# A two-layer hybrid decoder step on one core: two plain tile pairs open each feed-forward block, the first block's norm sums move into its third tile, and the embedding transposes move behind the gate's first tile

## The chip, the cores and the metric

The kernel runs on one core of one Trainium2 chip. Five engines run side by side, each with its own list of instructions in a fixed order: TensorE (PE in the profile, its weight loads PEld), VectorE (DVE), ScalarE (ACT), GpSimd (POOL) and SyncE (SP, which issues most DMAs here). [...] An engine that waits for one instruction's input holds back everything behind it in its own list. The metric is the device time of one execution in microseconds. The median of three runs is 2243.88 us (2239.72 to 2243.95).

## The reference

Two layers. Each layer is a feed-forward block with half weight, a mixing block (a state-space scan beside window attention), a second feed-forward block with half weight, and a gated per-layer embedding. 512 prompt tokens and 32 sample tokens go through together, 544 in all; the model is 1024 wide, the feed-forward blocks 2752.

```python
def _rmsnorm(x, w):
    y = xf * lax.rsqrt(jnp.mean(xf * xf, axis=-1, keepdims=True) + RMS_EPS)
    return (y * w).astype(x.dtype)

def _swiglu(x, w1, w3, w2):
    return (jax.nn.silu(x @ w1) * (x @ w3)) @ w2

h = h + 0.5 * _swiglu(_rmsnorm(h, g_ffn1), w1_a, w3_a, w2_a)
...
h = h + mix
h = h + 0.5 * _swiglu(_rmsnorm(h, g_ffn2), w1_b, w3_b, w2_b)
gate = sigmoid(_rmsnorm(h, g_ple) @ w_ple_gate)
h = h + gate * (pe @ w_ple_proj)
```

## The kernel before

The residual stream `h` stays in SBUF, 128 partitions by 8 chunks of 544 tokens. Every matrix product is made of three products of halves: an operand is split into a high part (a cast by ScalarE: `wh`, `qh`, `XH`) and the rest (a subtraction by VectorE: `wl`, `ql`, `XL`), and TensorE adds up high times high, high times low and low times high. A matmul has 272 columns, half of the tokens. So `xgemm`, one tile of 128 output columns over all 1024 inputs, is 8 x 3 x 2 = 48 matmuls, and the weights of each tile have to be loaded (`raw`), cast by ScalarE and subtracted by VectorE (`split`, L98 to L102) before they can be used.

**The norm.** `Norm` splits `h` times the gain into `XH` and `XL`. The factor of each token is applied later, to the products. GpSimd and ScalarE add up the squares into `acc`. `sums` (L166) lets TensorE add them over the partitions, VectorE makes `v` of them (L173, L174), and GpSimd raises it to the power -1/2 (`rt`, L175). `spread` (L177) lets TensorE copy the factors to all partitions, and ScalarE copies them to `Rb` (L184, L185). No product can be multiplied by its factor before `Rb` is there.

**A feed-forward block** (`ffn`) has 21 tile pairs and a remainder of 64 columns; a pair is 128 columns of w1 and the same 128 of w3. One pair and the remainder are computed plainly (`plain`): three `xgemm` tiles, `p1`, `p3` and the remainder `ps`. The other 20 pairs go through `pair`, which takes the four quarters of w1, w3 and of the input (two halves of the inputs by two halves of the tokens), and needs 7 products of quarters in place of 8. It pays with sums of weight quarters on VectorE and GpSimd (`q1` L338, L339, L340, L345), seven weight splits, and sums and differences of the results in VectorE (`v` L364 and L366, `c2`, `t`). A block pair is 84 matmuls; a plain pair is 96. The products read sums of input quarters that `block_sums` makes once for each block: ScalarE writes `Y`, VectorE makes four sums (L269 to L272), ScalarE casts them and VectorE subtracts (L276, L277), into `T` and into the part of `XH` and `XL` that the plain tiles have read. `Y` shares its buffers with `U`.

**Down.** The gated products go to sets `U` of four pairs. While the next set is computed, the down projection of the last one is added to `h`, two of eight output tiles for each pair: `plain_down` for the set of the plain pair and the remainder (10 matmuls and a weight unit of 2 x 128 columns for each tile), `down` for a set of four (24 matmuls and a weight unit of 4 x 128). So there are five sets of block pairs, and the first runs beside the small `plain_down`.

**Names for what follows.** I call the L366 instruction of a pair its second `v`. It frees the bank in which TensorE goes on (`T,wh` rows), so the distance from one second `v` to the next is the time of a pair. The stretch from the first tile of a block to its first second `v` is the opening. The blocks are counted FFN 1 to 4.

**The first block.** In layer 0 the tiles are begun while the input still comes in (`begun`); there the program calls `sums` after the second tile and `spread` after the third, while the other three blocks call them after the first and the second.

**The gate** (`ple`). `ple_prep` loads this layer's embedding `pt`, turns it with ten transposes on TensorE and splits it into `EH` and `EL`. It is called ahead of `ple`, so its transposes stand in TensorE's list ahead of the gate's first tile. The buffer of `pt` lies where the feed-forward block's buffers were, so its load waits for the end of that block. After the gate's first tile come `norm.sums`, the first projection of the embedding, and `norm.spread`.

**The order.** The code above is recorded, and a scheduling layer then sets the order of each engine's list; a list can therefore stand in another order than the code. Six `raw` buffers are shared by all weight units that are not `ra` (four more).

Of the kernel before, what the change touches and what calls it, by code (L numbers as in the profile page):

```python
# [9 lines left out]
F32 = mybir.dt.float32  # L10
F32R = mybir.dt.float32r
AF = mybir.ActivationFunctionType
ALU = mybir.AluOpType
# [3 lines left out]
DEPTH = 2  # L17
# [5 lines left out]
N = NP + NS  # L23
HN = N // 2
KU = 4
KD = DM // 128
# [13 lines left out]
def hymba_step(ctx: ExitStack, tc: tile.TileContext, I, O):  # L40
# [74 lines left out]
    def terms3(p, k, xh, xl):  # L115
        wh, wl = p[k // KU]
        k %= KU
        return [(wh[:, k, :], xh), (wh[:, k, :], xl), (wl[:, k, :], xh)]

    def gemm(groups):  # L120
        ps = (bank(), bank())
        n = len(groups)
        for gi, terms in enumerate(groups):
            for a in range(2):
                for i, (lhsT, rhs) in enumerate(terms):
                    PE.matmul(ps[a][:, 0:HN], lhsT, rhs[:, a * HN:(a + 1) * HN], start=gi == 0 and i == 0,  # L126
                              stop=gi == n - 1 and i == len(terms) - 1)
        return ps

    def xgemm(p):  # L130
        return gemm([[t for k in range(KD) for t in terms3(p, k, XH[:, k, :], XL[:, k, :])]])

    def xtile(w, c0):
        return xgemm(piece(w, 0, c0, KD))
# [99 lines left out]
    def ffn(g, w1, w3, w2, begun=None):  # L234
# [5 lines left out]
        with tc.tile_pool(name="ffn", bufs=2, reuse_waits="tile") as fp:  # L240
            T = fp.tile([128, 6, KU, HN], F32R, tag="T", name="T", bufs=1)

            def uset():
                return fp.tile([128, 2, PH, N], F32R, tag="U", name="U")

# [35 lines left out]

            def plain():
                U = uset()
                p1 = xgemm(first[0])
                if not begun:
                    norm.sums()
                p3 = xgemm(first[1])
                if begun:
                    norm.sums()
                else:  # L290
                    norm.spread()
                c0 = NJ * 128
                ps = xgemm(load_piece(
                    [(lambda t: t[:, :, 0:FREM], w1[:, c0:DFF].rearrange("(k p) m -> p k m", p=128)),
                     (lambda t: t[:, :, FREM:128], w3[:, c0:DFF].rearrange("(k p) m -> p k m", p=128))], KD))
                if begun:
                    norm.spread()
                sums = block_sums()
                s = act(p1)
                u = fp.tile([128, N], F32, tag="c2", name="u")  # L300
                for a in range(2):
                    V.tensor_tensor(u[:, HALF[a]], p3[a][:, 0:HN], s[:, HALF[a]], op=ALU.mult)
                keep(U, 0, u)
                b = fp.tile([64, N], F32, tag="c2", name="b64")
                for a in range(2):
                    A.copy(b[:, HALF[a]], ps[a][64:128, 0:HN])
                s = act(ps, 64)
                u = fp.tile([64, N], F32, tag="c2", name="ur")
                V.tensor_tensor(u, b, s[0:64, :], op=ALU.mult)
                A.copy(U[0:64, 0, 1, :], u)  # L310
                V.tensor_sub(U[64:128, 0, 1, :], u, U[0:64, 0, 1, :].bitcast(F32))
                return U, sums

            def plain_down(U, m):
                cs = slice(m * 128, (m + 1) * 128)
                parts = [(lambda t: t[:, 0, :], w2[0:128, cs])]
                parts += [(lambda t, a=a: t[a * 64:(a + 1) * 64, 1, :], w2[NJ * 128:DFF, cs]) for a in range(2)]
                p = split(raw_unit(parts), 2)
                terms = terms3([p], 0, U[:, 0, 0, :], U[:, 1, 0, :])
                terms += [(p[i][:, 1, :], U[:, 0, 1, :]) for i in range(2)]  # L320
                add_down(m, gemm([terms]), 0.25)

            def add_down(m, ps, f):
# [53 lines left out]
                V.tensor_tensor(c2, c2, th, op=ALU.mult)  # L377
                keep(U, i, c2)

            def down(j0, U, m):  # L380
                src = w2[j0 * 128:(j0 + PH) * 128, m * 128:(m + 1) * 128].rearrange("(k p) m -> p k m", p=128)
                p = load_piece([(lambda t: t, src)], PH)
                add_down(m, gemm([[t for k in range(PH) for t in terms3(p, k, U[:, 0, k, :], U[:, 1, k, :])]]), -0.25)

            U, sums = plain()
            last = lambda m, U=U: plain_down(U, m)
            for j0 in range(1, NJ, PH):
                U = uset()
                for i in range(PH):
                    pair(j0 + i, sums, U, i)  # L390
                    for m in range(2 * i, 2 * i + 2):
                        last(m)
                last = lambda m, U=U, j0=j0: down(j0, U, m)
            for m in range(KD):
                last(m)

# [734 lines left out]
    def ple(l, P, lp, E, last):  # L1131
        EH, EL = E
# [17 lines left out]
        for m in range(KD):  # L1150
            pg = xgemm(first if m == 0 else piece(wg, 0, m * 128, KD))
            if m == 0:
                norm.sums()
            p = piece(wpj, 0, m * 128, 2)
            pe = gemm([[t for k in range(2) for t in terms3(p, k, EH[:, k, :], EL[:, k, :])]])
            if m == 0:
# [43 lines left out]
    for l in range(DEPTH):  # L1200
# [7 lines left out]
        mix(l, P)  # L1208
        ffn(P["g2"], I["w1_b"][l], I["w3_b"][l], I["w2_b"][l])
        with tc.tile_pool(name="ple", bufs=2, reuse_waits="tile") as lp:  # L1210
            E = ple_prep(l, lp)
            Pn = params(l + 1) if l + 1 < DEPTH else None
            ple(l, P, lp, E, l == DEPTH - 1)
        P = Pn


# [62 lines left out]
```

## Time and profile before

| | |
|---|---|
| median of 3 runs | 2243.88 us |
| the profiled execution, its own time | 2237.84 us |
| its span | 2236.0 us |
| granted TensorE clock in that execution | 0.98 |
| DVE busy | 1808.7 us, 81% |
| ACT busy | 963.0 us, 43% |
| POOL busy | 701.2 us, 31% |

In the rows of the profile an engine's busy time is the union of its instructions. "x" is a count. A row of the stretches has for each engine the busy time and the number of instructions, then the granted TensorE clock, the busy share of the DMA engines, and GB/s. A row of a group has the line of the kernel, the engine, the operation, what it writes and reads, the shape, the count, the busy time, the mean ns of one, and the idle time before it with what ended it.

### The profile page before, as it was taken

The numbers are of one execution on the slowest core, as the hardware profiler recorded it, in microseconds if no ns is written. First come the engines' busy times: TensorE is split into PE (matmuls) and PEld (weight loads), VectorE is DVE, ScalarE is ACT, GpSimd is POOL, SyncE is SP. The second block draws the span as 40 slices with busy tenths as digits, with TensorE's granted clock in tenths as the row PEclk, the third lists the DMA queues.
The fourth block names the chain that finished last, engine by engine and source line by source line (L and its number), as shares of the span: only waits on it lengthen the run. The fifth ranks groups of instructions, "written<-read, shape, count | busy, mean of one in ns | idle before, by whom it ended". The sixth has DMA issues, their size and how long they took to land.

```text
span 2236.0 us, 43393 instructions
## 1 busy us (share of the span) xinstructions
PE 2132.3 (95%) x16706; PEld 2085.0 (93%) x16706; DVE 1808.7 (81%) x3282; ACT 963.0 (43%) x1784; POOL 701.2 (31%) x601
## 2 busy tenths in 40 slices
PE   7889999999999899999988999999999998999999
PEld 7889999998899899999988999999888888999998
DVE  7998987589878898986587889875987888988854
ACT  6344443444454444444363344443443543444343
POOL 5233331233533333322133333322334433323220
PEclk9999999999999999999999999999998999999999
DMA  5343332313252333332323333332223323333222
GB/s 143 101 118 95 91 104 72 80 50 86 58 139 63 99 95 100 91 90 73 87 64 100 101 95 92 93 81 70 59 76 90 94 74 104 91 103 96 77 70 76
DMA packets 401211, 197.89 MB, mean 88 GB/s; under 512 B 40270, under 2 KB 400358, under 8 KB 401004
## 3 DMA queue, kind: packets, MB, share of 16 engines
q1 hardware_dynamic: 399420, 194.93, 31.9%
q8 instruction: 132, 2.16, 0.4%
q14 instruction: 75, 0.61, 0.1%
q10 hardware_dynamic: 1584, 0.18, 0.0%
HBM read 187.56 MB, written 9.53 MB: 88 GB/s over the span
## 4 chain that ended last, share of the span: by engine, by line
PE 69%; DVE 18%; issue 4%; POOL 4%; DMA 3%; ACT 2%; POOLq 0%; SPq 0%; DVEq 0%; ACTq 0%
PE ps L126 35%; PE ps L354 28%; DVE wl L101 3%; DVE ql L101 2%; DVE CV L654 1%; POOL th L250 1%; DMA raw<-in_w_a 1%; POOL q L338 1%; DVE ra L345 1%; DMA raw<-in_w_b 1%; DVE wk L517 1%; PE ps L900 1%; DVE c L377 1%; DVE th L249 1%; POOL raw L339 1%
## 5 line engine op out<-in xcount | busy, mean ns | idle before, releaser
L126 PE MATMUL ps<-U,wh 128*128 128x272 f32 x2752 | 525.5, 288 | 0.0
L100 ACT CAST wh<-raw 128x512 fp32r<-128x512 f32 (+1 forms) x448 | 264.8, 596 | 445.6 <-PE ps L126 246.1
L126 PEld LDWEIGHTS ps<-U,wh 128*128 128x128 f32 x2752 | 434.4, 189 | 0.0
L126 PE MATMUL ps<-U,wl 128*128 128x272 f32 x1408 | 401.5, 288 | 0.0
L101 DVE TENSOR_TENSOR wl<-raw,wh 128x512 fp32r<-128x512 f32 (+1 forms) x448 | 312.9, 701 | 73.5 <-ACT wh L100 65.9
L126 PE MATMUL ps<-XH,wh 128*128 128x272 f32 x1184 | 352.3, 300 | 8.9 <-DVE wk L517 4.3
L126 PE MATMUL ps<-XL,wh 128*128 128x272 f32 x1184 | 345.8, 294 | 3.0 <-DVE XL L155 2.9
L126 PE MATMUL ps<-XH,wl 128*128 128x272 f32 x1152 | 336.9, 293 | 0.0
L126 PEld LDWEIGHTS ps<-U,wl 128*128 128x128 f32 x1408 | 265.4, 189 | 0.0
L354 PE MATMUL ps<-T,qh 128*128 128x272 f32 x1280 | 246.4, 289 | 0.5 <-ACT qh L100 0.4
L126 PEld LDWEIGHTS ps<-XH,wh 128*128 128x128 f32 x1184 | 227.8, 193 | 14.7 <-DVE wk L517 4.7
L338 POOL TENSOR_TENSOR q<-raw 128x512 f32<-128x512 f32 x80 | 124.9, 1561 | 355.0 <-DMA raw<-in_w_b 177.5
L126 PEld LDWEIGHTS ps<-XL,wh 128*128 128x128 f32 x1184 | 228.8, 193 | 4.8 <-DVE XL L155 4.3
L126 PEld LDWEIGHTS ps<-XH,wl 128*128 128x128 f32 x1152 | 222.6, 193 | 0.0
L375 POOL TENSOR_TENSOR t<-t,Rb 128x272 f32<-128x272 f32 x80 | 68.6, 857 | 463.2 <-DVE t L374 402.5
L354 PEld LDWEIGHTS ps<-T,qh 128*128 128x128 f32 x1280 | 202.0, 189 | 0.9 <-ACT qh L100 0.9
L354 PE MATMUL ps<-XH,wh 128*128 128x272 f32 x640 | 186.0, 291 | 11.3 <-ACT v L362 8.6
L354 PE MATMUL ps<-T,ql 128*128 128x272 f32 x640 | 186.1, 292 | 7.5 <-DVE ql L101 7.5
L354 PE MATMUL ps<-XH,ql 128*128 128x272 f32 x640 | 188.5, 294 | 4.1 <-DVE ql L101 4.1
L354 PE MATMUL ps<-XH,qh 128*128 128x272 f32 x640 | 187.8, 293 | 4.4 <-DVE c L368 4.4
L354 PE MATMUL ps<-XL,qh 128*128 128x272 f32 x640 | 188.4, 294 | 0.0
L101 DVE TENSOR_TENSOR ql<-ra,qh 128x512 fp32r<-128x512 f32 x160 | 181.9, 1137 | 7.7 <-ACT qh L100 0.7
(389 smaller groups left out, 5071.1 us busy)
## 6 DMA issues: line engine op xcount, KB each, us to landing
raw<-in_w_a SPq DMA_DIRECT2D x168, 256.0 KB
raw<-in_w_b SPq DMA_DIRECT2D x168, 256.0 KB
ra<-in_w_a SPq DMA_DIRECT2D x80, 256.0 KB
ra<-in_w_b SPq DMA_DIRECT2D x80, 256.0 KB
raw<-in_w_in SPq DMA_DIRECT2D x60, 256.0 KB
raw<-in_w_ple_gate SPq DMA_DIRECT2D x32, 256.0 KB
raw<-in_w_in SPq DMA_DIRECT2D x32, 128.0 KB
raw<-in_w_out SPq DMA_DIRECT2D x32, 128.0 KB
```

The costliest lines, as they stand in the source:

```text
L100: A.copy(wh[:, 0:n, :], raw[:, 0:n, :])
L101: V.tensor_sub(wl[:, 0:n, :], raw[:, 0:n, :], wh[:, 0:n, :].bitcast(F32))
L126: PE.matmul(ps[a][:, 0:HN], lhsT, rhs[:, a * HN:(a + 1) * HN], start=gi == 0 and i == 0, stop=gi == n - 1 and i == len(terms) - 1)
L249: V.scalar_tensor_tensor(th[0:np_, :], th[0:np_, :], 1.0, t1[0:np_, :], op0=ALU.add, op1=ALU.mult)
L250: G.tensor_tensor(th[0:np_, :], th[0:np_, :], Rb[0:np_, :], op=ALU.mult)
L338: G.tensor_tensor(q1, a21, a22, op=ALU.add)
L339: G.tensor_tensor(a21, a21, a11, op=ALU.add)
L345: V.tensor_tensor(a12, a12, a11, op=ALU.add)
L354: PE.matmul(ps[:, 0:HN], lhsT, rhs, start=start and k == 0 and n == 0, stop=k == KU - 1 and n == 2, skip_group_check=not start)
L375: G.tensor_tensor(t[:, HALF[1]], t[:, HALF[1]], Rb[:, HALF[1]], op=ALU.mult)
L377: V.tensor_tensor(c2, c2, th, op=ALU.mult)
L517: V.scalar_tensor_tensor(P3[:, kv, q, k0:256], sc[kv][:, q * 256:q * 256 + nk], rq[j][:, i, kv:kv + 1], bias_p[:, k0:256], op0=ALU.mult, o ...
```

## The change

It does three things.

1. `plain` computes two tile pairs plainly, pair 0 and pair 1. Its tiles are now `p1`, `p3`, `pn`, `pm` and the remainder. Nineteen pairs are left for `pair`, in sets of 3, 4, 4, 4 and 4. `plain_down` has three units of 128 rows of w2 (16 matmuls for each tile, before 10), the first `down` has three (18 matmuls, before 24), and the first set's three pairs share the eight `plain_down` tiles as 2, 3 and 3.
2. In the first block `sums` is called in the middle of the third tile, and `spread` behind it.
3. `ple_prep` is called behind the gate's first tile and its `sums`.

```diff
-    def gemm(groups):
+    def gemm(groups, mid=None):
         ps = (bank(), bank())
         n = len(groups)
         for gi, terms in enumerate(groups):
+            if gi and mid:
+                mid()
...
-    def xgemm(p):
-        return gemm([[t for k in range(KD) for t in terms3(p, k, XH[:, k, :], XL[:, k, :])]])
+    def xgemm(p, mid=None):
+        return gemm([[t for k in range(k0, k0 + KU) for t in terms3(p, k, XH[:, k, :], XL[:, k, :])]
+                     for k0 in range(0, KD, KU)], mid)
...
+                def product(i, p1, p3):
+                    s = act(p1)
+                    u = fp.tile([128, N], F32, tag="c2", name="u")
+                    for a in range(2):
+                        V.tensor_tensor(u[:, HALF[a]], p3[a][:, 0:HN], s[:, HALF[a]], op=ALU.mult)
+                    keep(U, i, u)
+
                 p1 = xgemm(first[0])
                 if not begun:
                     norm.sums()
                 p3 = xgemm(first[1])
                 if begun:
-                    norm.sums()
+                    pn = xgemm(piece(w1, 0, 128, KD), norm.sums)
+                    norm.spread()
                 else:
                     norm.spread()
+                    pn = xgemm(piece(w1, 0, 128, KD))
+                product(0, p1, p3)
+                pm = xgemm(piece(w3, 0, 128, KD))
                 c0 = NJ * 128
                 ps = xgemm(load_piece(
...
-                if begun:
-                    norm.spread()
+                product(1, pn, pm)
                 sums = block_sums()
-                s = act(p1)
-                u = fp.tile([128, N], F32, tag="c2", name="u")
-                for a in range(2):
-                    V.tensor_tensor(u[:, HALF[a]], p3[a][:, 0:HN], s[:, HALF[a]], op=ALU.mult)
-                keep(U, 0, u)
...
-            for j0 in range(1, NJ, PH):
+            for j0, n in ((2, PH - 1), (5, PH), (9, PH), (13, PH), (17, PH)):
                 U = uset()
-                for i in range(PH):
+                for i in range(n):
+                    ms = range(KD * i // n, KD * (i + 1) // n)
                     pair(j0 + i, sums, U, i)
-                    for m in range(2 * i, 2 * i + 2):
+                    for m in ms:
                         last(m)
...
             pg = xgemm(first if m == 0 else piece(wg, 0, m * 128, KD))
             if m == 0:
                 norm.sums()
+                EH, EL = ple_prep(l, lp)
...
-            E = ple_prep(l, lp)
```

The change moves the lists as follows at three places. Line numbers shift by up to ten (L101 stays; L173, L269, L366 become L176, L272, L375).

**VectorE at the opening of FFN 2.** Before, from the last weight split of the opening tiles on; `Y` and `T` are the sums of `block_sums`, `t_8495` is the first product times `Rb`:

```order
L101 TENSOR_TENSOR wl<-ra,wh 128x512
L271 TENSOR_TENSOR Y<-Y 128x4x272
L173 TENSOR_SCALAR v<-ps 128x4
L174 TENSOR_SCALAR v<-ps 32x1
L272 TENSOR_TENSOR Y<-Y 128x4x272
L277 TENSOR_TENSOR T<-Y,T 128x1088 x3
L340 TENSOR_TENSOR ra<-ra,q_8534 128x512
```

Now, from the same `v` on; `t_8461` and `t_8599` are the first products of the two plain pairs, times `Rb`:

```order
L177 TENSOR_SCALAR v<-ps 32x1
L101 TENSOR_TENSOR wl<-raw,wh 128x512 x3
L143 TENSOR_TENSOR t_8461<-ps,Rb 128x272 x2
L252 SCALAR_TENSOR_TENSOR th<-th,t_8461 128x544
L101 TENSOR_TENSOR wl<-ra,wh 128x512
L292 TENSOR_TENSOR u<-ps,th 128x272 x2
L143 TENSOR_TENSOR t_8599<-ps,Rb 128x272
L349 TENSOR_TENSOR ra<-ra,q_8659 128x512
L263 TENSOR_TENSOR U<-u,U 128x544
L143 TENSOR_TENSOR t_8599<-ps,Rb 128x272
L252 SCALAR_TENSOR_TENSOR th<-th,t_8599 128x544
L272 TENSOR_TENSOR Y<-Y 128x4x272
```

The sums of the input quarters stood ahead of the first product that needs `Rb`; now all of them stand behind the first plain pair and most of the second. FFN 3 and 4 have the same order.

**GpSimd at the opening of FFN 1 and FFN 2.** Before, in FFN 1, from the additions of squares to the power; `q_495` and `q_686` are weight sums of the first two block pairs, which read `raw` units:

```order
L164 TENSOR_TENSOR acc<-acc,sq 128x544 x4
L338 TENSOR_TENSOR q_495<-raw 128x512
L164 TENSOR_TENSOR acc<-acc,sq 128x544
L339 TENSOR_TENSOR raw<-raw,ra 128x512
L164 TENSOR_TENSOR acc<-acc,sq 128x544 x2
L338 TENSOR_TENSOR q_686<-raw 128x512
L175 TENSOR_TENSOR rt<-v,mhalf 128x5
```

Now, at the same place:

```order
L167 TENSOR_TENSOR acc<-acc,sq 128x544 x7
L347 TENSOR_TENSOR q_631<-raw 128x512
L348 TENSOR_TENSOR raw<-raw,ra 128x512
L178 TENSOR_TENSOR rt<-v,mhalf 128x5
L175 MEMSET v 128x1
```

The additions of squares are no longer broken up; the power still stands behind weight sums. In FFN 2 now (FFN 4 alike), `th` being the first plain pair's gate, which waits for `Rb`:

```order
L167 TENSOR_TENSOR acc<-acc,sq 128x544 x6
L178 TENSOR_TENSOR rt<-v,mhalf 128x5
L175 MEMSET v 128x1
L347 TENSOR_TENSOR q_8659<-raw 128x512
L348 TENSOR_TENSOR raw<-raw,ra 128x512
L347 TENSOR_TENSOR q_8862<-raw 128x512
L253 TENSOR_TENSOR th<-th,Rb 128x544
```

There the power stands ahead of all weight sums; before, four weight sums (L338 and L339, twice) stood ahead of it. The first gate stands behind the weight sum of the second block pair.

**TensorE at the gate of layer 0.** Before, from the last down matmul of FFN 2 to the gate's first tile (`XH`):

```order
L126 MATMUL ps<-U,wl 128x272
L1122 MATMUL ps<-ident,pt 128x128 x4
L1124 MATMUL ps<-ident,pt 128x32
L1122 MATMUL ps<-ident,pt 128x128 x4
L1124 MATMUL ps<-ident,pt 128x32
L193 MATMUL ps<-ident,pi 128x32
L126 MATMUL ps<-XH,wh 128x272
```

Now, from the last matmul of the gate's first tile on:

```order
L128 MATMUL ps<-XH,wl 128x272
L172 MATMUL ps<-ones,acc 128x1 x4
L172 MATMUL ps<-ones,acc 32x1
L1132 MATMUL ps<-ident,pt 128x128 x4
L1134 MATMUL ps<-ident,pt 128x32
L1132 MATMUL ps<-ident,pt 128x128 x4
L1134 MATMUL ps<-ident,pt 128x32
L128 MATMUL ps<-EH,wh 128x272 x2
```

The tile of 48 matmuls and the sums now stand ahead of the transposes; the first matmul on `EH` follows them at once.

More of the change, by code (lines that the diff above doesn't have):

```diff
@@ L309, in plain @@
                 V.tensor_tensor(u, b, s[0:64, :], op=ALU.mult)
-                A.copy(U[0:64, 0, 1, :], u)
-                V.tensor_sub(U[64:128, 0, 1, :], u, U[0:64, 0, 1, :].bitcast(F32))
+                A.copy(U[0:64, 0, 2, :], u)
+                V.tensor_sub(U[64:128, 0, 2, :], u, U[0:64, 0, 2, :].bitcast(F32))
                 return U, sums
@@ L315, in plain_down @@
                 cs = slice(m * 128, (m + 1) * 128)
[L316 to L320, printed above, removed]
+                parts = [(lambda t: t[:, 0:2, :], w2[0:256, cs].rearrange("(k p) m -> p k m", p=128))]
+                parts += [(lambda t, a=a: t[a * 64:(a + 1) * 64, 2, :], w2[NJ * 128:DFF, cs]) for a in range(2)]
+                p = split(raw_unit(parts), 3)
+                terms = [t for k in range(2) for t in terms3([p], k, U[:, 0, k, :], U[:, 1, k, :])]
+                terms += [(p[i][:, 2, :], U[:, 0, 2, :]) for i in range(2)]
                 add_down(m, gemm([terms]), 0.25)
@@ L378, in pair, with down @@
                 keep(U, i, c2)
[L380 to L383, printed above, removed]
+            def down(j0, n, U, m):
+                src = w2[j0 * 128:(j0 + n) * 128, m * 128:(m + 1) * 128].rearrange("(k p) m -> p k m", p=128)
+                p = load_piece([(lambda t: t, src)], n)
+                add_down(m, gemm([[t for k in range(n) for t in terms3(p, k, U[:, 0, k, :], U[:, 1, k, :])]]), -0.25)
             U, sums = plain()
             last = lambda m, U=U: plain_down(U, m)
-            for j0 in range(1, NJ, PH):
+            for j0, n in ((2, PH - 1), (5, PH), (9, PH), (13, PH), (17, PH)):
                 U = uset()
-                for i in range(PH):
+                for i in range(n):
+                    ms = range(KD * i // n, KD * (i + 1) // n)
                     pair(j0 + i, sums, U, i)
-                    for m in range(2 * i, 2 * i + 2):
+                    for m in ms:
                         last(m)
-                last = lambda m, U=U, j0=j0: down(j0, U, m)
+                last = lambda m, U=U, j0=j0, n=n: down(j0, n, U, m)
             for m in range(KD):
@@ L1129, in ple_prep, with ple @@
         return EH, EL
-    def ple(l, P, lp, E, last):
-        EH, EL = E
+    def ple(l, P, lp, last):
         wg, wpj = I["w_ple_gate"][l], I["w_ple_proj"][l]
@@ L1210, in hymba_step @@
         with tc.tile_pool(name="ple", bufs=2, reuse_waits="tile") as lp:
-            E = ple_prep(l, lp)
             Pn = params(l + 1) if l + 1 < DEPTH else None
-            ple(l, P, lp, E, l == DEPTH - 1)
+            ple(l, P, lp, l == DEPTH - 1)
         P = Pn
```

## The prediction

> **What bounds the kernel now.** I read the page's busy times first, then the steady part of one feed-forward block, then its openings and first pairs, and last the waits.
>
> ```profile
> span 2236.0 us, 43393 instructions
> PE 2132.3 (95%) x16706; PEld 2085.0 (93%) x16706; DVE 1808.7 (81%) x3282; ACT 963.0 (43%) x1784; POOL 701.2 (31%) x601
> 165.13 6.01 PE ps L126 x48
> 171.14 10.57 PE ps L354 x84
> 178.40:195.00 16.60, 16.60 (x135) 16.60 (x134) 14.91 (x25) 7.19 (x12) 5.29 (x4) 1.00 0.35 96
> ```
>
> TensorE is busy 95% of the span, so only what TensorE does not have to do, or no longer waits for, can pay. The last row is the time of one steady pair with its two down tiles: TensorE 16.60 of 16.60 us (84 block matmuls in 10.57, 48 down matmuls in 6.01), VectorE 14.91. There TensorE is the bound. The first six pairs of each block look different. These stretches run from the first to the seventh second `v` of FFN 1 to 4 (the first and seventh of FFN 2 stand below them):
>
> ```profile
> 56.80:161.40 104.60, 91.16 (x670) 89.19 (x670) 94.64 (x161) 40.10 (x75) 37.18 (x26) 0.95 0.37 106
> 701.00:801.30 100.30, 88.91 (x676) 86.73 (x675) 86.69 (x151) 40.72 (x76) 36.11 (x26) 0.98 0.32 90
> 1156.30:1261.90 105.60, 90.81 (x663) 89.27 (x664) 86.41 (x153) 39.78 (x75) 35.08 (x26) 0.94 0.34 93
> 1807.00:1907.20 100.20, 89.87 (x685) 87.91 (x684) 87.66 (x151) 40.49 (x76) 34.93 (x25) 0.98 0.33 90
> 701.04 0.42 DVE L366 TENSOR_TENSOR v<-v,ps 128x272 f32<-128x272 f32 x1
> 801.31 0.42 DVE L366 TENSOR_TENSOR v<-v,ps 128x272 f32<-128x272 f32 x1
> PE ps L354 <- DVE v L366: 27.5, 19, 3.6
> ```
>
> The last row is a wait over the whole span: total, times, longest. TensorE has less down work here than in the steady part, yet a pair takes 17 us, and TensorE is idle for 10 to 15 us of each stretch, most often for the second `v` of VectorE. So VectorE's list sets these stretches, and a block pair that leaves them takes VectorE's time with it.
>
> The openings, up to the same first second `v`:
>
> ```profile
> 14.20:56.80 42.60, 34.60 (x237) 32.67 (x235) 34.72 (x45) 27.70 (x49) 27.53 (x15) 0.92 0.42 106
> 668.00:701.00 33.00, 30.91 (x232) 30.29 (x230) 30.29 (x41) 19.27 (x33) 12.72 (x9) 0.95 0.21 57
> 1122.00:1156.30 34.30, 31.30 (x236) 29.60 (x235) 31.40 (x44) 23.62 (x40) 11.27 (x7) 1.00 0.24 66
> 1770.00:1807.00 37.00, 30.62 (x223) 29.64 (x223) 30.45 (x43) 19.78 (x34) 17.76 (x8) 0.91 0.19 50
> ```
>
> Both engines are busy for some 30 us of 33 to 37. An addition to either list makes them longer.
>
> **Part 1, the gates: -11.4 us.** The rows are of layer 0's gate, the first and third from the chain of work, two from the timeline, and last the wait over both gates.
>
> ```profile
> 1049.60 4.40 DMA pt<-in_p_prompt
> 1054.13 0.63 PE L1122 MATMUL ps<-ident,pt 128*128 128x128 f32 x4 [3.24 <-DMA pt<-in_p_prompt]
> 1056.40 8.53 PE ps L126 x48
> 1055.42 0.69 DVE L1127 TENSOR_TENSOR EL<-ps,EH 128x512 fp32r<-128x512 f32 x1 [1.81 <-ACT EH L1125]
> PE ps L1122 <- DMA pt<-in_p_prompt: 6.6, 2, 3.4
> ```
>
> The transposes head TensorE's list and wait 3.24 and 3.4 us for `pt`, which lands at 1054. The tile behind them takes 8.53 us where 48 matmuls took 6.01 at full clock, so the pause costs another 2.5. With the tile first, both go: 3.3 + 2.5 = 5.8. The transposes (1054.13 to 1056.40, 2.2 us) stay, but `pt` has long landed when the tile ends. What is added is that the first `EH` matmul follows the last transpose at once and needs a cast and a subtraction of the first half of `pt`. The subtraction ended at 1056.1, beside the transposes of the second half, so I take 0.1 of wait: -5.7 for each gate. Bounds for both gates: -12, and -9 with 1.3 us of wait in each (twice the 0.69 of the subtraction).
>
> **Part 2, the first pairs: -57.5 us.** One block pair less stands in each stretch: five distances in place of six, and all later pairs as before. By the steady row, VectorE's 25 instructions of 14.91 us are a pair's 18 and, for two down tiles, two splits and four additions to `h`, with one of a neighbour.
>
> ```profile
> L101 DVE TENSOR_TENSOR wl<-raw,wh 128x512 fp32r<-128x512 f32 x12 | 8.2, 682 | 0.0
> L366 DVE TENSOR_TENSOR v<-v,ps 128x272 f32<-128x272 f32 x6 | 2.6, 430 | 0.0
> ```
>
> With 0.68 for a split and 0.43 for a 272-column operation that is 14.91 - 2 x 0.68 - 5 x 0.43 = 11.4; I take 11.3. The first down tiles split 384 columns, not 256 (+0.5 a stretch). The idle time of VectorE in the stretch (its length less its busy time: 10.0, 13.6, 19.2, 12.5) falls by a sixth: 1.7, 2.3, 3.2, 2.1. So FFN 1 to 4 give 11.3 - 0.5 + a sixth = 12.5, 13.1, 14.0, 12.9, together **-52.5**. Behind it, the two down tiles of the set of three have 18 matmuls each in place of 24, and two of the pairs with them lie beyond the stretch: 12 matmuls x 6.01 / 48 = 1.5 at most, I take 1.3 a block: **-5**. Bounds of the -52.5: -45 (VectorE's 11.3 four times, no idle time) and -66 (the mean distance, 410.7 / 24 = 17.1, less 0.5, four times).
>
> **Part 3, the openings: +47 us.** Two more tiles are 96 matmuls, 12.0 us by the 6.01 row, where the pair that left had 10.57; on VectorE a plain pair is four splits and two short chains. But the order is the main thing. In FFN 2 these rows stood ahead of `Rb`, or behind it:
>
> ```profile
> 675.43 1.28 DVE L270 TENSOR_TENSOR Y<-Y 128x1088 f32<-128x1088 f32 x1
> 678.77 2.36 DVE L271 TENSOR_TENSOR Y<-Y 128x1088 f32<-128x1088 f32 x1
> 683.36 3.68 DVE L277 TENSOR_TENSOR T<-Y,T 128x1088 fp32r<-128x1088 f32 x3
> 688.21 0.58 ACT L184 COPY Rb<-ps 128x512 f32<-128x512 f32 x1
> 689.38 0.77 DVE L140 TENSOR_TENSOR t<-ps,Rb 128x272 f32<-128x272 f32 x2
> 691.28 0.71 DVE L249 SCALAR_TENSOR_TENSOR th<-th,t 128x544 f32<-128x544 f32 x1
> 694.19 0.79 DVE L302 TENSOR_TENSOR u<-ps,th 128x272 f32<-128x272 f32 x2 [1.26 <-POOL th L250]
> 696.43 0.72 DVE L260 TENSOR_TENSOR U<-u,U 128x544 fp32r<-128x544 f32 x1
> ```
>
> Before, seven of the eight sums were done when `Rb` came at 688.8, and the second `v` followed 12.2 us later. Now all eight stand behind the first product of the first plain pair, which needs `Rb`. VectorE's list from `Rb` to the second `v` is then: eight sums at 1.28 (10.2), two plain chains of 0.77 + 0.71 + 0.79 + 0.72 = 3.0 (6.0), the remainder's chain (2.9), seven splits and two weight sums at 0.68 (6.1), and two `v` and a `t` at 0.43 (1.3): 26.5 us. The waits for tanh, for GpSimd's `th` (1.26 above, three of them now) and between the late sums are 4 to 5. So the second `v` comes some 31 us behind `Rb`.
>
> ```profile
> 1138.78 0.58 ACT L184 COPY Rb<-ps 128x512 f32<-128x512 f32 x1
> 1792.97 0.59 ACT L184 COPY Rb<-ps 128x512 f32<-128x512 f32 x1 [5.89 <-PE ps L181]
> 1790.86 2.07 PE L181 MATMUL ps<-ident,rt 128*128 128x128 f32 x8 [4.62 <-POOL rt L175]
> 1780.18 7.83 POOL L338 TENSOR_TENSOR q<-raw 128x512 f32<-128x512 f32 x1 [7.79 <-PE ps L169]
> 41.70 0.59 ACT L184 COPY Rb<-ps 128x512 f32<-128x512 f32 x1
> PE ps L169 <- POOL acc L164: 3.8, 1, 3.8
> 32.45 7.58 POOL L175 TENSOR_TENSOR rt<-v,mhalf 128x5 f32<-128x5 f32 x1 [0.95 <-DVE v L174]
> 32.30:39.00 6.70, 6.70 (x36) 6.70 (x37) 6.67 (x8) 2.51 (x3) 6.55 (x1) 0.61 0.08 33
> ```
>
> FFN 2: L270 and L271 (3.6 us) no longer stand ahead of the second and third tiles' weights; TensorE's tiles let 1.5 of it through, so `Rb` comes at 687.3 and the second `v` at 718.4: +17.4. FFN 3: `Rb` 1139.4 as before, second `v` 1170.4: +14.1. FFN 4: the power `rt` stood behind a weight sum `q` of 7.83 us, and TensorE waited 4.62 for it; it now stands ahead, and sums on VectorE no longer delay `v`: `Rb` 7.2 earlier (4.62, and 2.6 for two sums of 1.28), at 1786.4, second `v` 1817.4: +10.4. FFN 1: the 3.8 us stall for `acc` goes since the sums come later; `rt`, which took 7.58, now stands behind `q_631` and the next addition, and I let the two come out even. So `Rb` comes at about 39, and behind it stand some 20 us of the same kinds (its weight splits stand ahead of `Rb`) and 3 of waits: 62, +5. Together **+47**. The lower bound is TensorE alone, three tiles, two more and the first 60 matmuls of a block pair (7.5 us) without a stall: I place that at +0.7, +11, +7.7 and +5, in all +24; the upper, with the waits I took doubled (5 us in four blocks), +65.
>
> As a check from the other side: a plain pair costs VectorE 5.1 us (four splits, four operations of 0.43, two of 0.72, less their overlap), so a block spares it 11.3 - 5.1 - 0.5 = 5.7 us and costs TensorE 1.45. My blocks gain 57.5 - 47 = 10.5, 2.6 each, which lies between.
>
> Where GpSimd and VectorE meet, a row is odd: `rt`, five columns, took 7.58 us while VectorE was busy for 6.67 of 6.70 us. [...]
>
> **The sum.** -11.4 - 57.5 + 47 = -22 against the profiled execution's 2237.84: 2216. The median of the runs is 6.04 above that execution, so 2243.88 - 22 = **2222**.
>
> **The rivals.** (a) The openings come down to TensorE's own time: +24 in place of +47, 2199, as its tiles hide what VectorE has behind `Rb`. For it: TensorE has 30.9 of 33.0 us to do there already. Against: the list behind `Rb`. (b) The blocks even out: idle time that leaves the stretch comes back in the opening. For it: TensorE's own work rises by 1.45 a block, and nothing but its idle time can shrink. If only the gates pay, it is 2243.9 - 11.4 = 2232. (c) The change does not do what it says: TensorE's 4 x 1.45 = 5.8 come on top, and behind the tile the transposes wait on their casts for 1.3 while the first tile still starts cold, so that a gate spares 3.3 - 1.3 = 2.0: 2243.9 + 5.8 - 4.0 = 2246, within 0.2%. (d) Slower: in the new openings GpSimd's first gate `th` stands behind `q_8862`, the second block pair's weight sum, whose `raw` buffer must be free and loaded.
>
> ```profile
> POOL q L338 <- DMA raw<-in_w_b: 177.5, 36, 8.9
> ```
>
> Such sums waited for their DMA 177.5 us in 36 cases, 8.9 at the longest. VectorE's `u`, and with it the whole list to the second `v`, would wait as well. It decides once each of four openings loses about 6 us (22 / 4); at 8.9 each, 36 us, the kernel is 13.6 slower on the sum, less what overlaps the waits I took: 2253. Against it: the plain tiles' loads stand ahead, and a `raw` buffer comes free with each split. (e) `rt` in FFN 1 is held as before, now behind `q_631`: five VectorE instructions on weights follow `v` without a break. Then `Rb` comes some 5 us later than I let it (7.58 less what it overlaps with), 2227. Against it: five splits of 0.68 are shorter than the 6.67 us of sums that lay beside it.
>
> **How the numbers follow.** Chances: forecast 0.42, (e) 0.05, (a) 0.16, (b) 0.17, (c) 0.08, (d) 0.12. A measurement of this kernel can tell 0.2%, 4.5 us, from no change. The forecast, (a), (b) and (e) are faster by more than that, 0.80; (c) is the same, 0.08; (d) is slower, 0.12. The forecast's own range is 2206 to 2232, from the bounds of parts 1 and 2 and a half of part 3's. The range that leaves out 2 in 10 goes from (a), 2198, to the lower edge of (c), 2244.
>
> **What would show it.** Right: the first second `v` of a block 48, 50, 48 and 47 us behind where the opening windows above begin (less what was gained ahead of it), with five following distances of 16 to 17.5 us; `rt` in FFN 4 ahead of `q`; no TensorE wait above 1 us for `pt`, and a first gate tile of 6.0. Wrong: `th` or `u` waiting for `q` on GpSimd; a stall at the first `EH`; distances that stay at six pairs' worth of time; a `spread` that waits in FFN 2 to 4.

## The result and the profile after

| | before | changed |
|---|---|---|
| median, first measurement (4 runs each) | 2242.15 us | 2219.88 us |
| median, second measurement (9 and 5 runs) | 2237.05 us | 2217.70 us |
| ratio, 95% interval | | 0.9918 (0.9897 to 0.9940); 0.9906 (0.9887 to 0.9924) |
| span of the profiled execution | 2236.0 us | 2217.8 us |

The changed kernel is 0.8 to 0.9% faster. The forecast was 2222 us. The head of the page of the changed kernel, to be held against the first two lines of the prediction:

```profile
span 2217.8 us, 43407 instructions
PE 2135.3 (96%) x16754; PEld 2088.9 (94%) x16754; DVE 1799.6 (81%) x3250; ACT 953.8 (43%) x1768; POOL 667.4 (30%) x589
```

TensorE has 48 matmuls more and is busy for 3.0 us more, but the span is 18.2 us shorter: only idle time has gone. The stretches of FFN 1 to 4 of the changed kernel, now from the first to the sixth second `v` (five distances, with the same 13 pairs left behind them; columns as before):

```profile
63.60:154.40 90.80, 83.29 (x617) 81.64 (x616) 79.69 (x136) 34.94 (x66) 31.30 (x23) 0.94 0.35 102
710.60:798.90 88.30, 81.37 (x612) 80.06 (x612) 82.06 (x134) 34.88 (x65) 29.65 (x22) 0.96 0.35 97
1159.50:1249.10 89.60, 81.06 (x612) 79.54 (x612) 81.85 (x133) 34.97 (x65) 30.15 (x22) 0.96 0.35 96
1805.60:1895.00 89.40, 81.33 (x612) 80.02 (x611) 82.51 (x133) 34.99 (x65) 29.69 (x22) 0.96 0.35 96
```

The first number behind the window is its length: 90.8 in place of 104.6, 88.3 of 100.3, 89.6 of 105.6, 89.4 of 100.2. TensorE's idle time in a stretch was 10.3 to 14.8 us (length less the first busy time) and is 6.9 to 8.5 us. The openings pay for it. In FFN 2, from the timeline of the changed kernel:

```profile
678.08 0.58 ACT L187 COPY Rb<-ps 128x512 f32<-128x512 f32 x1 [0.39 <-PE ps L184]
684.58 0.79 DVE L292 TENSOR_TENSOR u<-ps,th 128x272 f32<-128x272 f32 x2 [1.26 <-POOL th L253]
689.20 1.29 DVE L272 TENSOR_TENSOR Y<-Y 128x1088 f32<-128x1088 f32 x1
700.30 1.28 DVE L280 TENSOR_TENSOR T<-Y,T 128x1088 fp32r<-128x1088 f32 x1
699.24 0.64 PE L363 MATMUL ps<-T,qh 128*128 128x272 f32 x3 [1.00 <-DVE T L280]
710.46 0.36 PE L363 MATMUL ps<-XH,wh 128*128 128x272 f32 x1 [1.25 <-DVE v L373]
710.58 0.43 DVE L375 TENSOR_TENSOR v<-v,ps 128x272 f32<-128x272 f32 x1
```

`Rb` comes at 678.1, the first sum of the input quarters starts at 689.2 and the last ends at 701.6, TensorE waits for one of them, and the second `v` stands at 710.6, 32.5 us behind `Rb` where it was 12.8. The first gate `th` costs VectorE 1.26 us, as before; no weight sum holds it.

The gate of layer 0, first tile and then sums and transposes, in windows of the changed kernel:

```profile
1047.40:1053.40 6.00, 6.00 (x48) 6.00 (x49) 2.77 (x6) 1.98 (x4) 0.04 (x1) 1.00 0.43 136
1053.40:1056.00 2.60, 2.60 (x23) 2.15 (x21) 1.07 (x4) 1.40 (x4) 1.17 (x1) 1.00 0.27 80
```

The tile takes 6.00 us at a granted clock of 1.00, the transposes follow without a pause, and no wait for `pt` is left in the list of TensorE's waits, of which these bear on the change (total, times, longest):

```profile
PE ps L363 <- DVE v L375: 29.9, 21, 4.3
PE ps L363 <- DVE T L280: 2.9, 3, 1.0
PE ps L184 <- POOL rt L178: 2.2, 1, 2.2
PE ps L363 <- DVE XL L280: 1.3, 3, 0.4
PE ps L363 <- DVE ql L101: 0.7, 1, 0.7
```

The wait for the second `v` has stayed (27.5 before). What went are the waits for the splits `ql` of the first pairs (11.6 before, 0.7 now), for `pt` (6.6), for `acc` (3.8) and half of that for `rt` (5.1, 2.2). The waits for the sums `T` and `XL` are new.

### The profile page after: what moved, and what is told of

It is laid out like the page before. It is cut to its first block, busy times and chain, and to the rows that moved or that the text cites. A ratio compares the mean times of both kernels' runs of the same rounds, so it can differ in the third digit from the quotient of the medians.

```text
span 2217.8 us, 43407 instructions
## 1 busy us (share of the span) xinstructions
PE 2135.3 (96%) x16754; PEld 2088.9 (94%) x16754; DVE 1799.6 (81%) x3250; ACT 953.8 (43%) x1768; POOL 667.4 (30%) x589
## 3 DMA queue, kind: packets, MB, share of 16 engines
q8 instruction: 132, 2.16, 0.4%
## 4 chain that ended last, share of the span: by engine, by line
PE 49%; DVE 10%; issue 3%; ACT 1%; POOL 1%; DMA 1%; SPq 0%; ACTq 0%; DVEq 0%; POOLq 0%
PE ps L128 26%; PE ps L363 20%; DVE wl L101 3%; DVE ql L101 1%; DVE h L334 1%; POOL th L253 1%; DMA raw<-in_w_b 1%; DVE c L386 1%; ACT qh L100 0%; PE ps L910 0%; DVE T L280 0%; ACT U L262 0%; DVE CV L664 0%; DVE v L375 0%; DVE v L373 0%
## 5 line engine op out<-in xcount | busy, mean ns | idle before, releaser
L100 ACT CAST wh<-raw 128x512 fp32r<-128x512 f32 (+2 forms) x460 | 272.8, 597 | 482.3 <-PE ps L128 255.8
L101 DVE TENSOR_TENSOR wl<-raw,wh 128x512 fp32r<-128x512 f32 (+2 forms) x460 | 345.7, 756 | 84.6 <-ACT wh L100 76.3
L128 PE MATMUL ps<-XH,wh 128*128 128x272 f32 x1312 | 385.8, 296 | 9.1 <-ACT wk L552 5.3
L128 PE MATMUL ps<-XL,wh 128*128 128x272 f32 x1312 | 380.0, 291 | 1.8 <-DVE XL L158 1.6
L128 PE MATMUL ps<-XH,wl 128*128 128x272 f32 x1280 | 371.4, 291 | 0.0
L128 PEld LDWEIGHTS ps<-XH,wh 128*128 128x128 f32 x1312 | 249.2, 190 | 14.0 <-ACT wk L552 5.7
L128 PEld LDWEIGHTS ps<-XL,wh 128*128 128x128 f32 x1312 | 250.2, 191 | 3.7 <-DVE XL L158 3.3
L128 PEld LDWEIGHTS ps<-XH,wl 128*128 128x128 f32 x1280 | 243.6, 190 | 0.0
L347 POOL TENSOR_TENSOR q<-raw 128x512 f32<-128x512 f32 x76 | 107.1, 1409 | 314.2 <-DMA raw<-in_w_b 141.1
L363 PE MATMUL ps<-XH,wh 128*128 128x272 f32 x608 | 177.6, 292 | 14.5 <-ACT v L371 9.8
L253 POOL TENSOR_TENSOR th<-th,Rb 128x544 f32<-128x544 f32 (+1 forms) x88 | 129.1, 1467 | 179.6 <-DVE th L252 173.5
```

Source lines behind the costliest of these rows:

```text
L100: A.copy(wh[:, 0:n, :], raw[:, 0:n, :])
L101: V.tensor_sub(wl[:, 0:n, :], raw[:, 0:n, :], wh[:, 0:n, :].bitcast(F32))
L253: G.tensor_tensor(th[0:np_, :], th[0:np_, :], Rb[0:np_, :], op=ALU.mult)
L347: G.tensor_tensor(q1, a21, a22, op=ALU.add)
L363: PE.matmul(ps[:, 0:HN], lhsT, rhs, start=start and k == 0 and n == 0, stop=k == KU - 1 and n == 2, skip_group_check=not start)
```

## The experiments

Medians and ratios are against the kernel before on the same chip. Single executions scatter (29 of the kernel before lay between 2223 and 2251 us), so the intervals are near half a per cent wide; where a part of the program is meant, times between marked instructions of the profiled executions are compared.

### The gates alone

```diff
 def ple(l, P, lp, last):
             if m == 0:
                 norm.sums()
+                EH, EL = ple_prep(l, lp)
...
-            E = ple_prep(l, lp)
```

> The kernel before, with only the embedding transposes moved behind the gate's first tile. Theory (the wait for pt and the low clock behind it are the whole price, and they are independent of the feed-forward blocks): 11 us less than the kernel before, ratio 0.995; the first tile of each gate takes 6.0 us in place of 8.5. Rival (the gates' gain needs the blocks' new order, or the transposes only wait elsewhere): under 5 us.

Measured: 2229.68 us against 2240.18, ratio 0.9960 (0.9935 to 0.9986). In the profile, from the last second `v` of FFN 2 to the first of FFN 3 it is 135.15 us, 141.49 in the kernel before; from the last second `v` to the end 110.27, before 115.57. That is 6.3 + 5.3 = 11.6 us, with the blocks untouched. The theory stands.

### The pairs without the gates

```diff
+            E = ple_prep(l, lp)
...
             if m == 0:
                 norm.sums()
-                EH, EL = ple_prep(l, lp)
```

> The changed kernel, with the transposes back ahead of the gate. Theory (the parts add up): 11 us less than the kernel before as well, so 11 above the changed kernel; the four blocks keep their gain, about 49 us later openings against 57 to 60 us shorter stretches. Rival (the blocks even out and the gates give everything): within 4 us of the kernel before.

Measured: 2227.86 us, ratio 0.9947 (0.9926 to 0.9969), 12.3 below the kernel before. In this kernel's list of TensorE's waits the one for `pt` is back:

```profile
PE ps L1132 <- DMA pt<-in_p_prompt: 5.8, 2, 2.9
```

10.5 from the gates alone and 12.3 from the rest add up to 22.8; both together gave 22.3 and 19.4. The parts are independent within what the runs can tell. In this kernel's profile the openings are 44.9 us longer and the distances behind them 55.7 us shorter, a little less of each than expected.

One thing in the edit no run takes back alone: every `xgemm` tile is now two groups of 24 matmuls, one for each half of the inputs. In the gate of layer 1, which has eight such tiles, it changes nothing: from the last second `v` to the end it is 110.3 us in the changed kernel, and 110.27 with the gates alone, which have the old grouping.

### What the gate waited for

The embedding goes to three of the shared weight buffers, so that its load need not wait for the end of the block. The transposes stay where they were.

```diff
-        pt = lp.tile([128, 5, 256], F32, tag="pt", name="pt", bufs=1)
...
+        two = [raw_unit([(lambda t: t.rearrange("p (t s) c -> p t (s c)", t=2), src[:, i:i + 2, :])]) for i in (0, 2)]
+        two.append(raw_unit([(lambda t: t[0:NS, 0:2, :].rearrange("p s c -> p (s c)"), I["p_sample"][l].rearrange("b t c -> (b t) c"))]))
...
-                PE.transpose(p0[...], pt[:, t, c * 128:(c + 1) * 128], ident)
+                PE.transpose(p0[...], two[t // 2][:, 2 * (t % 2) + c, :], ident)
```

> The kernel before, with the embedding loaded into three of the shared weight buffers, which need not wait for the end of the feed-forward block; the transposes stay ahead of the gate's first tile. Theory (what is lost is the wait for pt's load, and the low clock is only its consequence): no TensorE wait for pt above 0.5 us, first tile near 6.0 us, 10 to 12 us less than the kernel before, as in the run with the transposes moved. Rival (ten short transposes ahead of the tile bring the low clock by themselves): the tile still takes over 8 us and only 6 to 7 us go. The load now stands ahead of weight loads in the shared buffers, which could cost up to 2 us.

Measured: 2227.30 us, ratio 0.9947 (0.9923 to 0.9971). The same two distances as above are 134.53 and 110.88, together 11.7 us less than before. Windows of the transposes and of the first tile of layer 0, first in the kernel before, then in this one:

```profile
1054.10:1056.40 2.30, 2.27 (x12) 1.67 (x12) 0.79 (x2) 0.99 (x3) 0.00 (x0) 0.62 0.00 0
1056.40:1064.90 8.50, 8.50 (x50) 8.50 (x51) 1.58 (x4) 1.04 (x4) 0.00 (x0) 0.70 0.00 0
```

```profile
1060.80:1062.30 1.50, 1.50 (x13) 1.12 (x12) 0.94 (x3) 1.11 (x4) 0.54 (x1) 1.00 0.45 129
1062.40:1068.60 6.20, 6.20 (x52) 6.19 (x50) 3.40 (x8) 2.36 (x5) 0.00 (x0) 1.00 0.43 127
```

The column behind the five engines is the granted clock: 0.62 and 0.70 behind the wait, 1.00 without it, with the transposes in the same place. So neither their place nor their kind cost anything. The pause did, once as idle time and once more as a slow tile. It can be removed by order or by an earlier load.

### The first block's sums

```diff
                 if begun:
-                    pn = xgemm(piece(w1, 0, 128, KD), norm.sums)
+                    norm.sums()
+                    pn = xgemm(piece(w1, 0, 128, KD))
                     norm.spread()
```

> The changed kernel, with the first block's sums back behind its second tile (the spread stays behind the third). Theory (the move inside the third tile only takes the wait for acc out of TensorE's list): TensorE waits some 3 to 4 us for acc ahead of the sums again, and the first block's first second v comes 2 to 4 us later than in the changed kernel; the total rises by 2 to 4. Rival (Rb is set by the power, and the opening by VectorE's list behind it, so TensorE's wait costs nothing): under 1 us.

Measured: 2219.45 us, ratio 0.9920 (0.9890 to 0.9951), the same as the changed kernel. In the profile of this run, the wait for `acc`, a later one of the first block pair, and the window behind it; last the same window of the changed kernel:

```profile
27.36 1.21 PE L172 MATMUL ps<-ones,acc 128*128 128x1 f32 x10 [0.92 <-POOL acc L167]
56.74 0.59 PE L364 MATMUL ps<-XH,wh 128*128 128x272 f32 x1 [4.32 <-ACT v L372]
56.74:62.60 5.86, 5.86 (x26) 5.86 (x27) 5.43 (x7) 4.02 (x6) 0.00 (x0) 0.50 0.01 3
```

```profile
56.51:62.25 5.74, 5.58 (x42) 5.36 (x43) 5.66 (x7) 3.92 (x6) 0.00 (x0) 1.00 0.01 3
```

The wait for `acc` is 0.9 us, not 3 to 4: GpSimd's additions were broken up by weight sums before, and no longer are. `Rb` comes even a little earlier (37.99 against 38.43), and still the first second `v` comes 2.5 us later (66.09 against 63.60). It isn't ScalarE's copy of `v` that holds it: that starts at 56.30, and at 56.07 in the changed kernel. TensorE reaches this wait 2 us earlier and so waits 4.32 us where it waited 2.11, and behind the wait it runs at a granted clock of 0.50 where it ran at 1.00, 26 matmuls in 5.9 us where 42 took 5.6. So the theory's 2 to 4 us were met at the first second `v`, but not by the wait it named. The total is 0.4 us below the changed kernel, in an interval of 7 us to either side: it can't tell the theory's 2 to 4 us from the rival's 1.

### Where the sums of the input quarters stand

`block_sums` is cut in two. What writes only `Y` and `T` is called ahead of the first product (first kernel) or behind it (second kernel); what writes into `XH` and `XL` stays behind the last plain tile.

```diff
+                t2, t3, t4 = (cast(y, T[:, 2 * i], T[:, 2 * i + 1]) for i, y in enumerate((y22, y12, y21)))
+                return lambda: [t2, t3, cast(y11, XH[:, 0:KU, HN:N], XL[:, 0:KU, HN:N]), t4]
...
+                late = block_sums()              # first kernel
                 product(0, p1, p3)
+                late = block_sums()              # second kernel
                 pm = xgemm(piece(w3, 0, 128, KD))
...
-                sums = block_sums()
+                sums = late()
```

> The changed kernel, with all sums of the input quarters but the one that writes XH and XL called ahead of the first product, so that VectorE makes them before Rb comes, as in the kernel before. Theory (the opening is set by VectorE's list behind Rb, 32.4 us in the changed kernel, of which 9 are these sums; TensorE has some 6 us of idle time there in FFN 2 to 4): the distance from Rb to the first second v falls by 5 to 6 us in FFN 2 to 4, Rb comes 1 to 2 us later, and the kernel is 10 to 18 us below the changed one. Rival (TensorE's five tiles set the opening, and early sums only delay the weights of the tiles and the norm's v): no less than the changed kernel, or more by up to 10.

> The changed kernel, with the same sums called behind the first product and ahead of the next tile, so that they stand behind Rb in VectorE's list but ahead of most of the second plain pair. Theory (what counts is what stands behind Rb): within 4 us of the changed kernel. Rival (the second plain pair in front of the sums is what holds them): 5 to 10 us less.

Measured: first kernel 2200.61 us against 2240.27, ratio 0.9829 (0.9805 to 0.9853); second 2224.36, ratio 0.9930 (0.9908 to 0.9953). Ahead of the first product the sums are worth about 20 us more than the change gave; behind it, nothing, as the theory of the second said. From `Rb` to the second `v` of FFN 1 to 4:

| | FFN 1 | FFN 2 | FFN 3 | FFN 4 |
|---|---|---|---|---|
| before | 15.1 | 12.8 | 17.6 | 14.0 |
| changed | 25.2 | 32.5 | 32.5 | 32.4 |
| sums ahead of the first product | 23.5 | 26.3 | 28.1 | 26.5 |
| sums behind it | 25.4 | 33.7 | 33.8 | 33.6 |

TensorE's work is the same in both, so VectorE's list behind `Rb` does hold the openings of the changed kernel above TensorE's own time: by the four openings (-3.5, -0.7, -4.0, -5.8) and the stretches (-2.1, -0.9, -1.3, -1.7) 20 us go. But TensorE isn't far behind. From `Rb` to the second `v` of FFN 4, first in the changed kernel, then in the first kernel here:

```profile
1773.18:1805.55 32.37, 29.52 (x215) 28.65 (x216) 25.04 (x38) 21.01 (x35) 8.95 (x5) 0.95 0.11 29
```

```profile
1761.45:1787.95 26.50, 26.07 (x206) 25.80 (x206) 23.91 (x36) 12.85 (x24) 8.11 (x5) 1.00 0.29 80
```

TensorE is busy for 29.5 of 32.4 us, part of it at the lower clock (0.95 on the mean), and then for 26.1 of 26.5: with the early sums it is the bound there.

FFN 2 gains least: there `Rb` comes 5.5 us later, as seen from the block ahead. The norm's `v` is done at 666.25, but in GpSimd's list a weight sum, which waited for its load and took 7.19 us, and the one behind it stand ahead of the power, and TensorE waits for that; rows of the first kernel's timeline:

```profile
666.11 0.14 DVE L177 TENSOR_SCALAR v<-ps 32x1 f32<-32x1 f32 x1
666.20 7.19 POOL L349 TENSOR_TENSOR q<-raw 128x512 f32<-128x512 f32 x1 [8.12 <-DMA raw<-in_w_b]
675.02 1.17 POOL L178 TENSOR_TENSOR rt<-v,mhalf 128x5 f32<-128x5 f32 x1
676.24 1.01 PE L184 MATMUL ps<-ident,rt 128*128 128x128 f32 x3 [4.04 <-POOL rt L178]
```

### The small set last

```diff
-            for j0, n in ((2, PH - 1), (5, PH), (9, PH), (13, PH), (17, PH)):
+            for j0, n in ((2, PH), (6, PH), (10, PH), (14, PH), (18, PH - 1)):
```

> The changed kernel, with the set of three pairs last instead of first, so that four pairs share the eight plain down tiles, two each, and the tiles of 18 matmuls come at the end of the block. TensorE's work is the same. Theory (the distances of 20 us behind the first second v are VectorE's, with three down tiles beside a pair): no distance over 18.5 us among the first four, TensorE's idle time in the stretch falls by 2 to 4 us a block, 8 to 16 us less than the changed kernel. Rival (the long distances are the backlog of the opening, and appear wherever the first pairs stand): within 4 us.

Measured: 2224.71 us, ratio 0.9934 (0.9910 to 0.9958): no gain. The distances behind the first second `v` of FFN 2 were 13.1, 20.2, 20.5, 18.1 and 16.5 us in the changed kernel, and are 15.4, 17.4, 20.1, 18.3 and 16.3 here. A long one is there still, one pair later. The stretches fall by 0.8 to 4.0 us, 8.5 in all, but the 13 distances behind them rise from 212.4 to 216.5 us in each block, as the last three pairs now share eight tiles of 24 matmuls (the last two distances are 17.6 and 18.3, before 14.8 and 16.4). The theory falls: a distance over 18.5 us is left, and nothing is won. The run moves tiles to the end of the block as well, so it doesn't price the three tiles alone. For the rival speaks the run with the early sums, in which the set of three still comes first: no distance of FFN 2 to 4 is over 18.7 us there.

### Three plain pairs

```diff
+                p5 = xgemm(piece(w1, 0, 256, KD))
+                product(1, pn, pm)
+                p6 = xgemm(piece(w3, 0, 256, KD))
...
-                product(1, pn, pm)
+                product(2, p5, p6)
...
-            for j0, n in ((2, PH - 1), (5, PH), (9, PH), (13, PH), (17, PH)):
+            for j0, n in ((3, PH - 2), (5, PH), (9, PH), (13, PH), (17, PH)):
```

> The changed kernel with a third plain pair in each block (sets of 2, 4, 4, 4 and 4, plain down tiles of 22 matmuls shared four and four by the first two pairs). Theory (a plain pair lengthens the opening by 12.5 us of TensorE and takes one VectorE-bound distance of 17 to 18 us with it): once more 3 to 5 us a block less than the changed kernel, 12 to 20 in all. Rival (there is no more idle time of TensorE to win, since two pairs that carry four down tiles each take 21 us of TensorE): within 4 us, or up to 10 us more.

Measured: 2195.28 us against 2240.27, ratio 0.9805 (0.9780 to 0.9830), some 25 us below the changed kernel, more than expected. The stretch of FFN 2 (now four distances), and the wait that ends its opening:

```profile
712.27:785.13 72.86, 71.49 (x554) 71.27 (x555) 63.63 (x112) 30.60 (x56) 21.34 (x17) 0.98 0.30 81
```

```profile
712.76 0.52 PE L366 MATMUL ps<-T,wh 128*128 128x272 f32 x2 [4.70 <-DVE v L378]
```

The stretch is 15.4 us shorter than that of the changed kernel, but TensorE's busy time in it only 9.9. The first two distances are 20.9 and 22.3 us, as the rival said, but without a pause: the down tiles of 22 matmuls fill the time in which TensorE waited for VectorE. The distance from `Rb` rises by 10.0 us in FFN 2, where the theory had 12.5 for the opening. Over the four blocks the openings grow by 38 us (9.5 each), and the stretches fall by 67 (16.7 each): the gain beyond the theory is that smaller growth.

### Both, and a place between

The early sums with three plain pairs (first kernel); the same sums behind the second product (second kernel). The changed kernel ran again beside them.

```diff
 first kernel
+                late = block_sums()
                 product(0, p1, p3)
 second kernel
                 product(1, pn, pm)
+                late = block_sums()
                 p6 = xgemm(piece(w3, 0, 256, KD))
```

> Three plain pairs and the early sums together. Theory (both win the same thing, TensorE's idle time in the openings and first pairs; with three plain pairs only 4.7 us of it is left, between Rb and the first second v of FFN 2 to 4): the gains don't add. 2 to 4 us a block at most, so 8 to 16 us below the run with three plain pairs (2195), and nothing if idle time comes back ahead of Rb, as it did in FFN 2 with the early sums. Rival (the gains are independent): 20 us below it, at 2175.

> Three plain pairs, with the sums called behind the second product and ahead of the third pair's second tile. They then stand behind Rb, where VectorE waits for tanh and for GpSimd, but ahead of the weights of the last two tiles. Theory (the 4.7 us wait of TensorE for the second v, from VectorE's list behind the last tile, goes, and nothing is added ahead of Rb): 3 to 4.5 us a block, 12 to 18 us below the run with three plain pairs. Rival (the sums now delay the last tiles' weights by as much): within 4 us of it.

> The changed kernel again, beside the two others on the same chip: 18 to 22 us below the kernel before if the first measurement holds, ratio 0.990 to 0.992.

Measured against 2237.05 us: both 2179.45, ratio 0.9734 (0.9715 to 0.9753); place between 2198.04, ratio 0.9818 (0.9800 to 0.9837); changed kernel again 2217.70, as in the table at the top. Both together are 16 us below three plain pairs alone, at the upper end of the theory: TensorE's 4.7 us wait for the first second `v` of FFN 2 is gone, and in exchange the `spread` waits ahead of `Rb` for a power that took 6.97 us:

```profile
663.30 6.97 POOL L178 TENSOR_TENSOR rt<-v,mhalf 128x5 f32<-128x5 f32 x1 [8.26 <-DVE v L177]
670.32 1.16 PE L184 MATMUL ps<-ident,rt 128*128 128x128 f32 x8 [1.15 <-POOL rt L178]
```

The rival's 2175 is only 4.5 us further down, about what the interval allows, so the median doesn't rule it out; the two profiled spans differ by 14.5 us, which is the theory's.

The place between gains nothing. TensorE waits as before, behind a list in which the sums still stand behind `Rb`:

```profile
716.01 0.59 PE L368 MATMUL ps<-T,wh 128*128 128x272 f32 x1 [3.90 <-DVE v L380]
```

The version with both is the fastest of this study, 2.7% below the kernel before.

## Why the prediction was right

The steps of the prediction against the two profiled executions. The openings are counted from the last second `v` of the block ahead; in FFN 3 the gate's 6.34 us, as the kernel with the gates alone has them, are taken out.

| step | predicted | measured |
|---|---|---|
| two gates | -11.4 | -6.34 - 5.31 = -11.7 |
| stretches (410.71 us before, 358.16 after) | -52.5 | -52.6 |
| 13 pairs behind them (853.54, 849.48) | -5 | -4.1 |
| openings of FFN 1 to 4 | +5, +17.4, +14.1, +10.4 = +47 | +6.8, +17.6, +13.3, +12.3 = +50.0 |
| sum | -22 | -18.3 |

The 47 is short by 3 here. In the second profiled execution of the changed kernel the openings are +53.0 (the last one +15.3), the stretches -54.0, and the sum is -16.1, so a term of this table is known to some 3 us.

**The gates** went as predicted, and the run with the earlier load shows that both halves of the price came from one wait. The wait added for `EH` was 0.2 us at most.

**The stretches** have the predicted sum, and nearly the predicted size block by block (92.1, 87.2, 91.6 and 87.4; measured 90.8, 88.3, 89.6 and 89.5). Their form was not as forecast. I expected distances of 16 to 17.5 us; measured in FFN 2 were 13.1, then 20.2 and 20.5. With the small set last the second distance falls from 20.2 to 17.4, but the third stays at 20.1; with the sums ahead of the first product all of FFN 2's are 16.5 to 18.7, while the five together change by only 0.9. So the long ones go with the late sums more than with the three down tiles. What a block pair costs was right on the mean, not one by one.

**The openings** came in part from the cause named. The order puts the sums behind the first product, and the run with the sums ahead of it takes 4.5 to 6.3 us off the distance from `Rb` in FFN 2 to 4. The openings are still 36 us longer there than before (+3.4, +16.8, +9.3, +6.5; in FFN 2 because of the late power). So 14 of the 50 us are shown to be the sums' place, and what stays in FFN 3 and 4 is near the prediction's bound of TensorE alone (+7.7 and +5). The term was short by 3: 31 us behind `Rb` were 32.4 to 32.5, and 23 in FFN 1 were 25.2. VectorE's work was counted well (26.5 us; 25.0 in the row of FFN 4 above), its waits were taken too low (4 to 5; 7.3). `Rb` itself came where it was put, within 2 us: in FFN 1 at 38.4 (forecast 39), in FFN 4 earlier by 6.0 (forecast 7.2), in FFN 2 by 2.1 (1.5).

**One step was wrong in its reason.** I let the first block's 7.58 us power and its place behind `q_631` "come out even". In the changed kernel:

```profile
29.17 1.10 PE L172 MATMUL ps<-ones,acc 128*128 128x1 f32 x10
31.82 0.95 DVE L101 TENSOR_TENSOR wl<-raw,wh 128x512 fp32r<-128x512 f32 x1 [2.81 <-ACT wh L100]
34.23 0.13 DVE L177 TENSOR_SCALAR v<-ps 32x1 f32<-32x1 f32 x1
34.44 1.18 POOL L178 TENSOR_TENSOR rt<-v,mhalf 128x5 f32<-128x5 f32 x1 [0.53 <-DVE v L177]
35.68 2.07 PE L184 MATMUL ps<-ident,rt 128*128 128x128 f32 x8 [2.20 <-POOL rt L178]
```

GpSimd was free and waited 0.53 us for `v`, and the power took 1.18 us, 6.4 less than before. But `v` came 2.0 us later than before: TensorE's sums were done at 30.27, and in VectorE's list `v` stood behind a weight split that waited 2.81 us for ScalarE. From the power to `Rb` it is 1.1 us more. So `Rb` came 3.3 us earlier, where 2.7 were forecast, by other terms than the prediction's; that it came out so close was luck.

**The rivals.** Openings at TensorE's own time (a) did not happen here, but the runs with early sums come near to it, and that is where their gain lies. The blocks did not even out (b): without the gates the change still gives 12 us. (c) fell with the first gate's tile at a granted clock of 1.00 and no wait for `EH` above 0.2 us. Nothing waited for `q_8862` (d): the wait for `th` is the 1.26 us that stood there before. The first power was not held (e).

## What to carry to other kernels

Where a stretch is held by one engine and the next engine has idle time, work that moves from the first to the second pays even if it is more in all: here 1.45 us more of TensorE a block took 13 us out of the stretch and put 12.5 us into the opening, and the third plain pair took out 16.7 and put in 9.5. Price such a move by the whole distance that goes, the held engine's idle time included, and by what the opening grows; and look at the list behind the value that everything waits for: work that does not need it should stand ahead of it. And ask of a short wait what clock the work behind it runs at, since the wait may cost its own length once more (here 3.1 us behind a wait of 3.24).

## What was not expected of the hardware

In the gate of layer 0 a wait of 3.24 us of TensorE was followed by 10.8 us at a granted clock of 0.62 and 0.70; without the wait the same 58 matmuls and transposes took 7.7 us at 1.00. The loss behind the wait, 3.1 us, was as large as the wait; in the gate of layer 1 it was 1.9 (5.3 less the wait of 3.4). The kernel before shows the difference: TensorE was busy without a break behind both waits, but the granted clock was 0.50 over the whole of a window of 6.74 us at the first and of 3.40 us at the second. Half of each is my estimate of the loss, 3.4 and 1.7 us.

```profile
1054.66:1061.40 6.74, 6.74 (x30) 6.25 (x30) 1.68 (x5) 1.35 (x4) 0.00 (x0) 0.50 0.00 0
2160.60:2164.00 3.40, 3.40 (x15) 2.97 (x15) 1.58 (x4) 1.31 (x4) 0.00 (x0) 0.50 0.03 5
```

In the traces of the kernel before and the changed one, 19 and 15 spells at a granted clock of 0.50 are 3.41 us long (12 and 7 of them), 6.83 (5 and 5) or 13.65 (1 and 2), but for the last one of each trace, which the end of the program breaks off. What makes it 3.41 or 6.83 here is not shown.

The first power on GpSimd, five columns, took 7.58 us in the kernel before, while VectorE was busy for 6.67 of 6.70 us beside it. With the gates alone and with the earlier load one instruction kept GpSimd busy at that place for 7.19 and 7.35 of 7.50 us. In the changed kernel, in its repetition and with the sums at the place between, the first power took 1.18 us, though it is the first one of the execution in all of them: the difference, 7.58 - 1.18 = 6.4 us, is not a price of being first. Nor is it only the first power: in the run with three plain pairs and the early sums the first one took 2.16 us, and those of FFN 2 (above) and FFN 4 took 6.97:

```profile
1738.61 6.97 POOL L178 TENSOR_TENSOR rt<-v,mhalf 128x5 f32<-128x5 f32 x1 [8.25 <-DVE v L177]
```

In the kernel before, two of GpSimd's powers and weight sums took over 4 us: that first power, and the weight sum of 7.83 us at 1780.18. Both ended 1.1 us behind the first pause in VectorE's list beside them (at 38.97 and 1786.87; the two ended at 40.03 and 1788.01). In the changed kernel none took over 4 us. What holds them is not shown: no run changed VectorE's list beside them alone.
